# Delta scan: one chain of four heads on halves and quarters of the array, without zero padding

## The chip, the cores and the metric

The kernel runs on one core of a Trainium2 chip. The metric is the device time of one execution in microseconds (us): median of several runs. The core has a matrix engine (PE in the profile; PEld are its weight loads), a vector engine (DVE), a scalar engine (ACT), GpSimd (POOL) and a queue engine (SP) that issues DMAs. Lnnn is a line of the kernel before; lines of the changed kernel are marked as such.

## The reference

Two layers; each joins two branches that run along 512 tokens of 2048 channels. The change lies in branch A, a gated delta rule over chunks of 64 tokens, for 8 heads of 128 channels, once forwards and once backwards:

```python
def step(S, xs):
    q_c, k_c, u_c, w_c, g_c, qk_c = xs
    v_new = u_c - jnp.einsum('bhck,bhkv->bhcv', w_c, S)
    o_c = (jnp.einsum('bhck,bhkv->bhcv', q_c * jnp.exp(g_c)[..., None], S)
           + jnp.einsum('bhcs,bhsv->bhcv', qk_c, v_new))
    g_last = g_c[..., -1:]
    S = (S * jnp.exp(g_last)[..., None]
         + jnp.einsum('bhck,bhcv->bhkv', k_c * jnp.exp(g_last - g_c)[..., None], v_new))
    return S, o_c
```

`u_c` and `w_c` come from a triangular solve over the chunk; the kernel holds the inverse of that triangle times beta (`T` below) and applies it to `v - k S`. All else in a layer is large dense products: the input projection, the gated unit and projection of branch B, the merge and the output projection.

## The kernel before, in words

Dense products keep 128x128 weights in the array and stream 512 tokens. Each is three passes in split precision (L122, L123, L124), one contraction tile after another; a tile's three matmuls are called a **fill step** here. Eight weight tiles at a time come by DMA (`w_raw`), ACT makes their high part (L65) and DVE their low part (L66).

The scan, `_delta_scan`, runs over 16 steps in each layer: two groups of four heads, and eight steps `j` in each. In a step the forward direction (`d = 0`) takes chunk `j` and the backward one chunk `7 - j`; one of them lies on partitions 0 to 63 of its 128-token tile, the other on 64 to 127 (`half[d]`). Each group is split into two chains, `x = 0, 1`, of two heads. A step does, for each chain and both directions:

- **ps_T** (L807): (q | k) times the state `S`, four float32 matmuls on the whole array into one PSUM bank. Each float32 matmul stands as two instructions in the trace.
- **r_s** (L810): DVE, `v - k S`, one instruction of 64x256 for each direction. Then the state is decayed (L813, 128x512).
- **ps_V** (L821): `T` times `r_s`, two matmuls with 128 rows. `T` holds both directions' 64x64 blocks on the diagonal, zeros beside them.
- **v_z** (L824): ACT copies the new values out of PSUM, each direction to a tile of its own whose other half is zero.
- **ps_S** (L831): keys times new values, four matmuls with 128 rows of which 64 meet zeros. DVE adds them to the state (L836).
- **outputs** (L839): `a_s` times new values onto ps_T, four matmuls of 128 rows and 64 columns, into the half of the partitions of their direction. ACT copies them out while `j < 4` (L844), after that DVE adds them (L846).

The order on PE is written by hand (`manual_schedule`); each `fill.run(FILL)` puts three fill steps into it: one after the ps_T of both chains, one after both ps_V, one at the step's end. So a step has nine fill steps, 27 dense matmuls. Fill steps come from the last two of the 48 z products and from branch B's gated unit and projection; those that the scan leaves over run after it. Other engines' order is the scheduler's, with weight splits and epilogues of dense products at high priority. When a group is done, `norm` makes its head norms on ACT and DVE, and its heads leave PE by transposes, one a step (`late`).

The inputs of the scan are written to DRAM in `_delta_pre` and `_delta_inv` and loaded by the POOL queue (`load`).

Of the kernel before, what the change touches and what calls it, by code (L numbers as in the profile page):

```python
# [15 lines left out]
F32 = mybir.dt.float32  # L16
# [12 lines left out]
NH = 8  # L29
# [13 lines left out]
FILL = 3  # L43
# [4 lines left out]
# The order of the first three products.  x: loads an input tile; h: its two parts; s: its squares;  # L48
# w j,k,n: weights of product j from contraction tile k on; p j,n: the next n steps of product j.
# [31 lines left out]
def _dense(c, w, nk, hi, lo):  # L81
    """PSUM [128, 512] = w.T @ act over nk contraction tiles; w is a DRAM view [128, nk, 128]."""
# [8 lines left out]
def _weights(c, w):  # L91
    """hi and lo parts of up to eight weight tiles."""
# [10 lines left out]
class _Fill:  # L103
    """Dense products in small steps, for the places where another chain waits."""
# [11 lines left out]
def _steps(c, acc, nk, unit, hi, lo):  # L116
    """acc = w.T @ act, one contraction tile at a time; unit gives the weights from a tile on."""
# [17 lines left out]
def _sum_sq(c, ps, acc, t0, n, first):  # L135
    """Adds the sums of acc over partitions, token tiles t0 to t0 + n, onto the columns of ps [token, tile]."""
# [13 lines left out]
def _spread(c, pb, r, n):  # L150
    """pb [any partition, token] = r [token, tile]."""
# [4 lines left out]
def _rstd(c, acc, out):  # L156
    """out = (sum of acc over partitions / D + eps) ** -0.5 on every partition."""
# [8 lines left out]
def _scaled_parts(c, x, g, hi, lo):  # L166
    """Splits x*g into hi, lo."""
# [4 lines left out]
def _add_squares(c, pool, k, x, acc):  # L172
    """Adds x*x onto acc."""
# [84 lines left out]
        # c.gtok: [token in tile, t, row]; rows 0-7/32-39 exp(tot - gc), rows 64-71/96-103 g  # L258
# [9 lines left out]
def _halves(c, out, w, x, start, stop):  # L268
    """out [128, n] = w.T @ x by halves of the columns of the array, side by side."""
# [27 lines left out]
def _sincos(nc, pool, s_out, c_out, x, tag):  # L297
    """sin and cos of x by quarter turns and polynomials."""
# [18 lines left out]
    # quadrant q = n mod 4 from f = n/4 - round(n/4) in {-1/2, -1/4, 0, 1/4, 1/2}:  # L317
    # cos(pi n / 2) = 1 - 4|f| on those points, sin(pi n / 2) = sign of f on odd n
# [6 lines left out]
    # sin(pi n / 2) = 4 f (1 - cq^2)  # L325
# [13 lines left out]
def _s5(ctx, c, l):  # L339
    """S5 scan in chunks of 8 tokens; partitions are (lag, channel) or (re|im, state)."""  # L340
# [5 lines left out]
    for hf in range(2):  # L346
        with ExitStack() as es:
# [12 lines left out]
            with tc.tile_pool(name=f"s5p_{l}_{hf}", bufs=1, reuse_waits="tile") as pp:  # L360
# [17 lines left out]
                # (lam_bar - 1) / lam  # L378
# [13 lines left out]
                # b_bar: rows (re, im); b_in[0] = (b_re, b_im), b_in[1] = (b_im, b_re)  # L392
# [12 lines left out]
                # powers 0..8  # L405
# [23 lines left out]
            def gen(out, a, p, b, q, gs, d, ks, kn):  # L429
                """out [128, 4, kn, 16] = a*p + b*q over lags ks (a slice)."""  # L430
# [12 lines left out]
            # chunk inputs of the state: forward into slot n + 1, backward into slot n  # L443
# [41 lines left out]
            def kernels(jl):  # L485
                """What the outputs of a channel tile need besides the states."""
# [28 lines left out]
                # M[(s, c'), g, t, c] = K[c', g, t - s, c]  # L515
# [40 lines left out]
def _qk_norms(c, ss):  # L556
    """Inverse norms, by tokens, from the sums of squares ss [(t, k heads | q heads), token in tile]."""
# [47 lines left out]
def _delta_pre(c, l):  # L605
# [4 lines left out]
    with tc.tile_pool(name=f"dp_{l}", bufs=1, side="right", reuse_waits="tile") as wk, \  # L610
            tc.tile_pool(name=f"pp_{l}", bufs=1, space=PSUM, side="right", reuse_waits="tile") as pp:
        for h in range(NH):
            # decay factors [(chunk parity, s), direction, t, c], masked
            ps = c.psq.tile(W, F32, name="ps_d", tag="psq")
            for d in range(2):
                # tri[k, c] g[k]: k <= c forward, k >= c backward
# [15 lines left out]
            for d in range(2):  # L632
# [4 lines left out]
                # columns of chunk n: (q_e | k_e) for even n, (k_e | q_e) for odd n  # L637
# [5 lines left out]
                # in the order in which the direction takes the chunks  # L643
                nc.scalar.copy(out=c.egl[:, d, h, ::1 - 2 * d], in_=pe[:, last:SEQ:CH])
# [19 lines left out]
            for d in range(2):  # L664
# [3 lines left out]
                c.q.dma_start(out=c.d_kd[l][d, :, :, h, :].rearrange("t p x -> p t x"), in_=kd)  # L668
# [36 lines left out]
def _delta_scan(c, l, fill):  # L705
    """Both directions over the chunks, in two groups of four heads, each as two chains of two heads."""
# [3 lines left out]
    NC = 2  # L710
    with ExitStack() as es:
# [3 lines left out]
        tb = [tp.tile([128, 4, 128], F32, name=f"t_b{q}") for q in range(2)]  # L715
        # new values, zero in the half of the other direction
        vz = [[[tp.tile([128, 2, 128], F32, name=f"v_z{x}{d}{p}") for p in range(2)] for d in range(2)] for x in range(NC)]
        Sg = [[tp.tile([128, 2, 2, 128], F32, name=f"s_st{hg}{x}") for x in range(NC)] for hg in range(2)]
# [556 lines left out]
```

## Time and profile before

| | |
|---|---|
| median of 3 runs | 3102.72 us (3102.61 to 3102.72) |
| span of the profiled execution, first to last instruction | 3099.7 us |
| PE, DVE, ACT, POOL busy | 3049.4, 2307.3, 1049.6, 425.6 us |
| scan matmuls, both layers: L831, L807, L839, L821 | 61.9, 54.9, 41.2, 34.7 us |

The profiled execution is told by its span alone; its whole device time, with what lies around the span, is not in the record. The median of the runs is 3.0 us above the span. In the views, a row of the timeline merges neighbours of one line: start, time from the first start to the last end, engine, line, operation, tiles, array shape, operand, count, and in brackets the idle time before. Matmuls are pipelined, so one matmul's duration is longer than the distance to the next: distances between starts are what a block costs.

### The profile page before, as it was taken

To read this page: it belongs to the slowest core of one execution; us is meant where nothing else is said; L and a number is where in the kernel's file an instruction comes from. 1 tells how busy PE (TensorE), PEld (TensorE's weight loads), DVE (VectorE), ACT (ScalarE), POOL (GpSimd) and SP (SyncE) were. 2 spreads that over 40 slices of the span, in tenths; PEclk is the share of its full clock that TensorE was granted. 3 is DMA by queue.
4 is the path that set the end of the run, shared out by engine and by line. 5 is a ranking of instruction groups with operands and counts; after the bars stand their busy time and mean duration, and the time that the engine had idled before them with its cause. 6 is when DMAs were issued, how large, how long until landed. Compare 5 with 4: busy or idle time off the path is not lost.

```text
span 3099.7 us, 45254 instructions
## 1 busy us (share of the span) xinstructions
PE 3049.4 (98%) x17142; PEld 2442.4 (79%) x17142; DVE 2307.3 (74%) x4455; ACT 1049.6 (34%) x1441; POOL 425.6 (14%) x706
## 2 busy tenths in 40 slices
PE   9999999999999999999999999999999999999998
PEld 7777788777887888888887677877778878888887
DVE  8899969997797586543487998889959965765433
ACT  4343344333222442322223334343332224423222
POOL 1010112212101231000010102022130012300000
PEclk9999999999999999999999999999999999999999
DMA  6343446755434765754433435466564356657433
GB/s 204 93 140 105 129 153 179 214 168 157 153 119 149 223 195 178 245 169 143 148 112 96 129 103 150 137 195 193 166 181 139 119 188 191 201 187 232 154 117 114
DMA packets 199289, 493.47 MB, mean 159 GB/s; under 512 B 58336, under 2 KB 62912, under 8 KB 198048
## 3 DMA queue, kind: packets, MB, share of 16 engines
q1 hardware_dynamic: 154416, 345.84, 35.1%
q0 software_dynamic: 44512, 144.74, 15.3%
q8 instruction: 135, 2.21, 0.3%
q14 instruction: 82, 0.67, 0.1%
q10 hardware_dynamic: 144, 0.01, 0.0%
HBM read 381.64 MB, written 108.86 MB: 158 GB/s over the span
## 4 chain that ended last, share of the span: by engine, by line
PE 83%; DVE 11%; issue 3%; DMA 1%; ACT 0%; POOL 0%; SPq 0%; POOLq 0%; DVEq 0%; ACTq 0%
PE acc L122 24%; PE acc L123 24%; PE acc L124 24%; DVE w_lo L66 2%; PE ps_y L271 2%; PE ps_S L831 2%; PE ps_T L807 1%; DVE st_b L482 1%; DVE st_b L481 1%; DVE h_st L484 1%; PE ps_e L271 1%; DVE cv_y L550 1%; PE ps_et L457 1%; PE ps_T L839 1%; DVE st_a L483 1%
## 5 line engine op out<-in xcount | busy, mean ns | idle before, releaser
L122 PE MATMUL acc<-act,w_hi 128*128 128x512 f32 x3200 | 1279.0, 400 | 5.5 <-DVE cv_pre L546 3.7
L124 PE MATMUL acc<-act,w_lo 128*128 128x512 f32 x3200 | 1271.6, 397 | 3.5 <-DVE w_lo L66 3.5
L123 PE MATMUL acc<-act,w_hi 128*128 128x512 f32 x3200 | 1269.6, 397 | 0.0
L65 ACT CAST w_hi<-w_raw 128x1024 fp32r<-128x1024 f32 (+1 forms) x467 | 488.2, 1046 | 1202.1 <-PE acc L123 879.9
L66 DVE TENSOR_TENSOR w_lo<-w_raw,w_hi 128x1024 fp32r<-128x1024 f32 (+1 forms) x465 | 566.7, 1219 | 266.5 <-ACT w_hi L65 264.3
L122 PEld LDWEIGHTS acc<-act,w_hi 128*128 128x128 f32 x3200 | 603.0, 188 | 150.4 <-issue 8.4
L124 PEld LDWEIGHTS acc<-act,w_lo 128*128 128x128 f32 x3200 | 602.7, 188 | 149.4 <-issue 7.0
L123 PEld LDWEIGHTS acc<-act,w_hi 128*128 128x128 f32 x3200 | 603.3, 189 | 138.4 <-issue 5.1
L122 PE MATMUL acc<-m_l,w_hi 128*128 128x512 f32 (+1 forms) x528 | 205.0, 388 | 0.0
L123 PE MATMUL acc<-m_h,w_hi 128*128 128x512 f32 (+1 forms) x528 | 204.8, 388 | 0.0
L124 PE MATMUL acc<-m_h,w_lo 128*128 128x512 f32 (+1 forms) x528 | 204.7, 388 | 0.0
L550 DVE SCALAR_TENSOR_TENSOR cv_y<-cv_pre,cw,cv_y 128x510 f32<-128x510 f32 (+1 forms) x192 | 142.6, 746 | 7.5 <-ACT cv_y L548 5.5
L122 PEld LDWEIGHTS acc<-m_l,w_hi 128*128 128x128 f32 x528 | 99.5, 188 | 21.9
L123 PEld LDWEIGHTS acc<-m_h,w_hi 128*128 128x128 f32 x528 | 99.5, 188 | 21.8
L124 PEld LDWEIGHTS acc<-m_h,w_lo 128*128 128x128 f32 x528 | 99.5, 188 | 21.8
L693 DVE TENSOR_TENSOR x_tmp<-x_inv 128x62 f32<-128x62 f32 (+30 forms) x124 | 106.3, 857 | 2.9
L695 DVE TENSOR_TENSOR x_inv<-x_inv,x_tmp 128x62 f32<-128x62 f32 (+30 forms) x124 | 106.3, 857 | 2.7
L1072 DVE TENSOR_TENSOR z_t<-acc,rstd_b 128x512 f32<-128x512 f32 x96 | 66.0, 687 | 48.2 <-PE acc L124 47.6
L1158 DVE TENSOR_TENSOR x_res<-x_res,acc 128x512 f32<-128x512 f32 x31 | 21.3, 687 | 103.7 <-PE acc L124 86.5
L1142 DVE TENSOR_TENSOR g_in<-acc,g_in 128x512 f32<-128x512 f32 x32 | 22.1, 692 | 79.4 <-PE acc L124 79.4
L518 POOL DMA_DIRECT2D m_l<-d_k x128 | 67.3, 534 | 82.2 <-PE ps_y L271 56.1
L484 DVE TENSOR_TENSOR h_st<-h_st,st_a 128x64 f32<-128x64 f32 x256 | 70.3, 275 | 5.1
(356 smaller groups left out, 3251.0 us busy)
## 6 DMA issues: line engine op xcount, KB each, us to landing
w_raw<-in_w_in_dram SPq DMA_DIRECT2D x319, 512.0 KB, 4.0
w_raw<-in_w_out_dram SPq DMA_DIRECT2D x64, 512.0 KB, 3.9
d_keqe<-k_e POOLq DMA_DIRECT2D x32, 512.0 KB, 4.5
d_g<-z_t SPq DMA_DIRECT2D x64, 256.0 KB, 2.1
w_raw<-in_w_pb_dram SPq DMA_DIRECT2D x32, 512.0 KB, 3.7
g_in<-d_g SPq DMA_DIRECT2D x64, 256.0 KB, 3.1
w_raw<-in_w_pa_dram SPq DMA_DIRECT2D x32, 512.0 KB, 4.3
ke_s<-d_keqe POOLq DMA_DIRECT2D x56, 256.0 KB, 4.1
```

The source lines that it names most:

```text
L65: nc.scalar.copy(out=hi, in_=src)
L66: nc.vector.tensor_tensor(out=lo, in0=src, in1=hi.bitcast(F32), op=ALU.subtract)
L122: c.nc.tensor.matmul(acc, wh[:, q, :], lo(k), start=k == 0, stop=False)
L123: c.nc.tensor.matmul(acc, wh[:, q, :], hi(k), start=False, stop=False)
L124: c.nc.tensor.matmul(acc, wl[:, q, :], hi(k), start=False, stop=k == nk - 1)
L271: c.nc.tensor.matmul(out[r], w[:, r], x, start=start, stop=stop)
L484: V.tensor_tensor(out=hs(n + 1), in0=hs(n + 1), in1=a, op=ALU.add)
L518: c.q.dma_start(out=M[s_ * 16:(s_ + 1) * 16].rearrange("p g t c -> p g (t c)"), in_=c.d_k[l][j][:, :, 0:16, (7 - s_) * 16:(15 - s_) * 16]. ...
L550: nc.vector.scalar_tensor_tensor(out=y[:, o0:o1], in0=pre[:, i0:i0 + o1 - o0], scalar=cw[:, tap:tap + 1], in1=y[:, o0:o1], op0=ALU.mult, o ...
L693: V.tensor_tensor(out=t, in0=_bc(X[:, k + 1:, k:k + 1], [128, n, k]), in1=_bc(X[:, k:k + 1, 0:k], [128, n, k]), op=ALU.mult)
L695: V.tensor_tensor(out=X[:, k + 1:, 0:k], in0=X[:, k + 1:, 0:k], in1=t, op=ALU.add)
L1072: V.tensor_tensor(out=z, in0=acc, in1=c.rstd, op=ALU.mult)
```

## The change

The two chains become one chain of four heads, with one ps_T of two banks, one `r_s`, one ps_V, one state. Heads 2 and 3 of a group take the other half of the rows: `_delta_pre` writes their `a` and keys (`kd`) with the halves of the partitions swapped, each as two DMAs where one was (`store`). With that

- ps_V multiplies 64x64 blocks alone, eight matmuls for four, of 64 rows and 64 columns: at each `q` the four of them stand on four different quarters of the array;
- ps_S has 64 rows, eight matmuls as before, alternating between the two halves of the rows, whose sums go to different banks;
- the outputs have 64 rows and 64 columns, eight matmuls as before, four to a round on four quarters;
- `T` and the new values have no zero half any more, and the memsets of 10 tiles on POOL in each layer go;
- ACT copies the new values in one instruction of 128x512 for eight of 64x256 in a step (four in each chain); DVE's `r_s` is two of 64x512 for four of 64x256, the decay one of 128x1024 for two of 128x512, the additions to the outputs two of 64x512 for four of 64x256;
- the fill steps stand 2, 3, 4 in the three places instead of 3, 3, 3.

```diff
-FILL = 3
+FILLS = (2, 3, 4)
...
+        def store(out, x):
+            if h % 4 < 2:
+                c.q.dma_start(out=out, in_=x)
+            else:
+                c.q.dma_start(out=out[64:128], in_=x[0:64])
+                c.q.dma_start(out=out[0:64], in_=x[64:128])
...
-                c.q.dma_start(out=c.d_a[l][d, :, :, h, :].rearrange("t p c -> p t c"), in_=at[:, d])
+                store(c.d_a[l][d, :, :, h, :].rearrange("t p c -> p t c"), at[:, d])
...
-        tb = [tp.tile([128, 4, 128], F32, name=f"t_b{q}") for q in range(2)]
...
-            nc.gpsimd.memset(q, 0.0)
...
-            T = tb[p]
+            T = wk.tile([128, H4, CH], F32, name="t_i", tag="t_i")
...
+        def lanes(x, d):
+
+            e = x[:, d, 0:1, 0:1]
+            n = x.ap[1][0]
+            return bass.AP(tensor=e.tensor, offset=e.offset,
+                           ap=[list(x.ap[0]), [n * (1 - 2 * d) + 256, 2], [128, 2], [1, 128]])
...
-                        for h in range(2):
-                            nc.tensor.matmul(ps[:, d, h, :], ke[d][:, 2 * x + h, :], S[x][:, d, h, :],
-                                             start=d == 0 and h == 0, stop=True, skip_group_check=True)
+            systems = [(e, q, e if q < 2 else 1 - e) for q in range(H4) for e in range(2)]
+            ps = psp.tile([128, 2, H4, 128], F32, name="ps_T", tag="T")
+                for e, q, d in systems:
+                    nc.tensor.matmul(ps[:, e, q, :], ke[d][:, q, :], S[:, e, q, :],
+                                     start=q == 0, stop=True, skip_group_check=True)
...
+                    V.tensor_tensor(out=r[half[d]].rearrange("p (z h) x -> p z h x", z=2),
+                                    in0=v.rearrange("p (z h) x -> p z h x", z=2),
+                                    in1=lanes(ps[half[1 - d]], d), op=ALU.subtract)
...
+                V.tensor_tensor(out=S, in0=S, in1=_bc(c.egl[:, hg, :, :, j:j + 1], [128, 2, H4, 128]), op=ALU.mult)
+            fill.run(FILLS[0])
...
-                    nc.tensor.matmul(pv[:, h, :], T[:, 2 * x + h, :], rr[x][:, h, :], start=True, stop=True)
+            for q in range(2):
+                for h in (q, q + 2):
+                        nc.tensor.matmul(pv[half[d if h < 2 else 1 - d], d, q, :], T[half[d], h, :], r[half[d], h, :],
+                                         start=True, stop=True)
+            vv = wk.tile([128, 2, 2, 128], F32, name="v_n", tag="v_n")
+            nc.scalar.copy(out=vv, in_=pv[:, :, 0:2, :])
+            fill.run(FILLS[1])
...
-                            nc.tensor.matmul(ps[:, d, h, :], ld[d][1][:, 2 * x + h, :], vv[x][d][:, h, :],
-                                             start=True, stop=True)
+                for e, q, d in systems:
+                    nc.tensor.matmul(pS[:, e, q, :], ld[d][1][half[e], q, :], vv[half[e], d, q % 2, :],
+                                     start=True, stop=True)
...
-                        nc.tensor.matmul(pT[x][half[d], d, h, :], ld[d][0][:, 2 * x + h, :],
-                                         vv[x][d][:, h, :], start=j == 0 and h == 0, stop=True, skip_group_check=True)
+            for q in range(2):
+                for e, p, d in systems:
+                    if p % 2 == q:
+                        nc.tensor.matmul(ps[half[d], e, p, :], ld[d][0][half[e], p, :], vv[half[e], d, p % 2, :],
+                                         start=j == 0 and p in (0, 2), stop=True, skip_group_check=True)
...
-            fill.run(FILL)
+            fill.run(FILLS[2])
```

On PE, the state updates and outputs of the first step of the first layer stand like this before (`v_z` with different numbers are the chains and directions, `kd_s` and `a_s` with different numbers the directions; x2 are two matmuls):

```order
L831 MATMUL ps_S_9418<-v_z_9329,kd_s_9357 128x128 x2
L831 MATMUL ps_S_9418<-v_z_9331,kd_s_9363 128x128 x2
L839 MATMUL ps_T_9375<-v_z_9329,a_s_9359 64x128
L839 MATMUL ps_T_9375<-v_z_9331,a_s_9365 64x128
L839 MATMUL ps_T_9375<-v_z_9329,a_s_9359 64x128
L839 MATMUL ps_T_9375<-v_z_9331,a_s_9365 64x128
L831 MATMUL ps_S_9430<-v_z_9333,kd_s_9357 128x128 x2
L831 MATMUL ps_S_9430<-v_z_9335,kd_s_9363 128x128 x2
L839 MATMUL ps_T_9379<-v_z_9333,a_s_9359 64x128
```

and in the changed kernel (its L835 are the state updates, its L845 the outputs):

```order
L835 MATMUL ps_S<-v_n,kd_s_9350 128x128
L835 MATMUL ps_S<-v_n,kd_s_9356 128x128
L835 MATMUL ps_S<-v_n,kd_s_9350 128x128
L835 MATMUL ps_S<-v_n,kd_s_9356 128x128 x2
L835 MATMUL ps_S<-v_n,kd_s_9350 128x128
L835 MATMUL ps_S<-v_n,kd_s_9356 128x128
L835 MATMUL ps_S<-v_n,kd_s_9350 128x128
L845 MATMUL ps_T<-v_n,a_s_9352 64x128
L845 MATMUL ps_T<-v_n,a_s_9358 64x128 x2
L845 MATMUL ps_T<-v_n,a_s_9352 64x128 x2
L845 MATMUL ps_T<-v_n,a_s_9358 64x128 x2
L845 MATMUL ps_T<-v_n,a_s_9352 64x128
```

Two blocks of state updates and two of outputs in turn have become one of each.

On DVE, between the state updates of step `j = 4` of the first group and the subtraction of the next step, the rows before are these (`act`, `z_in` and `glu_s` belong to the gated unit of branch B):

```order
L836 TENSOR_TENSOR s_st_9337<-s_st_9337,ps_S_9869 128x512
L846 TENSOR_TENSOR o_tok_9341<-o_tok_9341,ps_T_9806 64x256 x2
L1099 TENSOR_TENSOR z_in<-z_in,glu_s 128x8x64
L836 TENSOR_TENSOR s_st_9338<-s_st_9338,ps_S_9881 128x512
L846 TENSOR_TENSOR o_tok_9342<-o_tok_9342,ps_T_9815 64x256 x2
L66 TENSOR_TENSOR act_9724<-z_in,act_9722 128x512
L810 TENSOR_TENSOR r_s_9921<-v_s_9660,ps_T_9920 64x256
L810 TENSOR_TENSOR r_s_9921<-v_s_9666,ps_T_9920 64x256
```

and in the changed kernel (its L841, L1105, L852, L816 and L820 are L836, L1099, L846, L810 and L813 before):

```order
L841 TENSOR_TENSOR s_st_9343<-s_st_9343,ps_S 128x512 x2
L1105 TENSOR_TENSOR z_in<-z_in,glu_s 128x8x64
L852 TENSOR_TENSOR o_tok_9345<-o_tok_9345,ps_T 64x512 x2
L66 TENSOR_TENSOR act_9718<-z_in,act_9716 128x512
L816 TENSOR_TENSOR r_s<-v_s_9637,ps_T 64x512
L816 TENSOR_TENSOR r_s<-v_s_9643,ps_T 64x512
L820 TENSOR_TENSOR s_st_9343<-s_st_9343,egl 128x1024
```

The additions to the outputs now all stand behind both state additions, and the whole of the next step's ps_T, which reuses the same two banks, waits for them; before, each chain had a ps_T bank of its own.

## Rows read from the trace of the kernel before

**Rows 1.** Page, part 1: busy time and share of each engine, instructions.

```profile
PE 3049.4 (98%) x17142; PEld 2442.4 (79%) x17142; DVE 2307.3 (74%) x4455; ACT 1049.6 (34%) x1441; POOL 425.6 (14%) x706
```

**Rows 2.** Timeline of PE, one scan step of the first layer (`j = 1` to `j = 2`).

```profile
1038.99 1.05 PE L821 MATMUL ps_V<-r_s,t_b 128*128 128x128 f32 x8
1039.80 0.48 PE L122 MATMUL acc<-act,w_hi 128*128 128x512 f32 x1
1040.12 0.39 PE L123 MATMUL acc<-act,w_hi 128*128 128x512 f32 x1
...
1041.98 1.05 PE L831 MATMUL ps_S<-v_z,kd_s 128*128 128x128 f32 x8
1042.96 0.66 PE L839 MATMUL ps_T<-v_z,a_s 128*64 128x128 f32 x8
1043.55 1.16 PE L831 MATMUL ps_S<-v_z,kd_s 128*128 128x128 f32 x8
...
1045.23 0.50 PE L122 MATMUL acc<-act,w_hi 128*128 128x512 f32 x1
1045.56 0.40 PE L123 MATMUL acc<-act,w_hi 128*128 128x512 f32 x1
...
1047.42 1.95 PE L807 MATMUL ps_T<-s_st,ke_s 128*128 128x128 f32 x16
```

**Rows 3.** Timeline of PE, the last step of a group: both chains' outputs together.

```profile
1116.16 1.09 PE L839 MATMUL ps_T<-v_z,a_s 128*64 128x128 f32 x16
```

**Rows 4.** Timeline of PE, 32-column matmuls of branch B between dense ones.

```profile
198.62 0.42 PE L508 MATMUL ps_k<-c_l,b_bar 128*32 128x128 f32 x8
...
215.64 0.40 PE L122 MATMUL acc<-act,w_hi 128*128 128x512 f32 x1
215.97 0.64 PE L508 MATMUL ps_k<-c_l,b_bar 128*32 128x128 f32 x16
216.54 0.50 PE L123 MATMUL acc<-act,w_hi 128*128 128x512 f32 x1
```

**Rows 5.** Line L839: weight loads of the outputs, shortest, median and longest ns.

```profile
L839 PEld LDWEIGHTS ps_T<-v_z,a_s x512: 132/137/137, 1030.6 to 2756.0; 128*64 128x64 f32 x171
```

**Rows 6.** DVE's groups, 1020 to 1240 us: busy, mean ns, idle before, releaser.

```profile
L66 DVE TENSOR_TENSOR w_lo<-w_raw,w_hi 128x1024 fp32r<-128x1024 f32 x24 | 29.4, 1223 | 23.0 <-ACT w_hi L65 23.0
L810 DVE TENSOR_TENSOR r_s<-v_s,ps_T 64x256 f32<-64x256 f32 x56 | 23.5, 420 | 14.1 <-PE ps_T L807 12.6 <-DMA a_s<-d_a 0.2
L836 DVE TENSOR_TENSOR s_st<-s_st,ps_S 128x512 f32<-128x512 f32 x24 | 16.4, 685 | 17.1 <-PE ps_S L831 16.9
L1099 DVE TENSOR_TENSOR z_in<-z_in,glu_s 128x512 f32<-128x512 f32 x8 | 9.3, 1168 | 0.1
```

**Rows 7.** Timeline of PE and DVE around three subtractions.

```profile
1035.11 1.95 PE L807 MATMUL ps_T<-s_st,ke_s 128*128 128x128 f32 x16
1036.75 0.85 DVE L810 TENSOR_TENSOR r_s<-v_s,ps_T 64x256 f32<-64x256 f32 x2
...
1134.46 0.87 DVE L810 TENSOR_TENSOR r_s<-v_s,ps_T 64x256 f32<-64x256 f32 x2
1135.38 0.71 PE L821 MATMUL ps_V<-r_s,t_b 128*128 128x128 f32 x4 [0.56 <-DVE r_s L810]
...
2698.70 1.95 PE L807 MATMUL ps_T<-s_st,ke_s 128*128 128x128 f32 x16
2700.13 0.86 DVE L810 TENSOR_TENSOR r_s<-v_s,ps_T 64x256 f32<-64x256 f32 x2
```

**Rows 8.** Waits of PE over the whole span: total us, times, longest.

```profile
PE ps_V L821 <- DVE r_s L810: 2.8, 4, 0.8
```

**Rows 9.** Timeline, first layer: the scan's first load on POOL, its first ps_V.

```profile
996.95 0.54 POOL L743 DMA_DIRECT2D v_s<-d_v  x1 [7.08 <-DMA d_ti<-l_in]
...
1026.68 1.05 PE L821 MATMUL ps_V<-r_s,t_b 128*128 128x128 f32 x8
```

**Rows 10.** POOL's groups over the whole span: the stores of the keys.

```profile
L668 POOL DMA_DIRECT2D d_kd<-k_d x32 | 24.0, 753 | 32.4 <-DVE k_d L666 21.2 <-DVE st_a L483 6.6 <-DMA m_l<-d_k 1.7
```

More of the change, by code (lines that the diff above doesn't have):

```diff
@@ L642, in _delta_pre @@
                 last = CH - 1 if d == 0 else 0
-                nc.scalar.copy(out=c.egl[:, d, h, ::1 - 2 * d], in_=pe[:, last:SEQ:CH])
+                nc.scalar.copy(out=c.egl[:, h // 4, d if h % 4 < 2 else 1 - d, h % 4, ::1 - 2 * d], in_=pe[:, last:SEQ:CH])
                 c.q.dma_start(out=c.d_keqe[l][d, :, :, h, :].rearrange("n p x -> p n x"),
@@ L667, in _delta_pre @@
                                 in1=_bc(c.gtok[:, :, 32 * d + h:32 * d + h + 1], [128, 4, 128]), op=ALU.mult)
-                c.q.dma_start(out=c.d_kd[l][d, :, :, h, :].rearrange("t p x -> p t x"), in_=kd)
+                store(c.d_kd[l][d, :, :, h, :].rearrange("t p x -> p t x"), kd)
 def _delta_inv(c, l):
@@ L749, in load @@
             for d in range(2):
[L750 to L752 removed]
+                c.q.dma_start(out=T[half[d]], in_=c.d_ti[l][d, hs, n_[d]].rearrange("h s c -> s h c"))
             return T, ke, dict(token)
         def norm(hg):
[L757 to L783 removed]
@@ L784, in norm @@
-            return late
+            ot = og[hg]
+            ms = tp.tile([128, 4, H4], F32, name=f"o_ms{hg}")
+            for t in range(4):
+                sq = wk.tile([128, H4, 128], F32, name="o_sq", tag=f"o_sq{t % 2}", bufs=1)
+                nc.scalar.activation(out=sq, in_=ot[:, t], func=AF.Square)
+                V.tensor_reduce(out=ms[:, t], in_=sq, axis=AX.X, op=ALU.add)
+            rq = c.rq[:, :, hg * 4:hg * 4 + 4]
+            f = tp.tile([128, 4, H4], F32, name=f"o_f{hg}")
@@ new lines, in norm @@
+            V.tensor_tensor(out=f, in0=rq, in1=rq, op=ALU.mult)
+            V.tensor_tensor(out=f, in0=f, in1=ms, op=ALU.mult)
+            V.tensor_scalar(out=f, in0=f, scalar1=1.0 / 128, scalar2=EPS, op0=ALU.mult, op1=ALU.add)
+            _rsqrt(nc, tp, ms, f, f"o_rt{hg}")
+            V.tensor_tensor(out=f, in0=ms, in1=rq, op=ALU.mult)
+            for h in range(0, H4, 2):
+                V.tensor_tensor(out=ot[:, :, h:h + 2], in0=ot[:, :, h:h + 2],
+                                in1=_bc(f[:, :, h:h + 2].unsqueeze(3), [128, 4, 2, 128]), op=ALU.mult)
@@ new lines, in head @@
+            def head(h):
+                pt = c.psq.tile([128, 4, 128], F32, name="ps_o", tag="psq")
+                for t in range(4):
+                    nc.tensor.transpose(pt[:, t, :], ot[:, t, h, :], c.ident)
+                of = wk.tile([128, 4, 128], F32, name="o_t", tag=f"o_sq{h % 2}", bufs=1)
+                nc.vector.tensor_scalar(out=of, in0=pt, scalar1=c.hng, scalar2=None, op0=ALU.mult)
+                c.q.dma_start(out=c.d_o[l][hg * 4 + h], in_=of.rearrange("p t x -> p (t x)"))
@@ L786, in _delta_scan @@
+            return [lambda h=h: head(h) for h in range(H4)]
+        def lanes(x, d):
[3 more added lines that the diff above has]
+                           ap=[list(x.ap[0]), [n * (1 - 2 * d) + 256, 2], [128, 2], [1, 128]])
         late = []
@@ L847, in _delta_scan @@
-            fill.run(FILL)
+            systems = [(e, q, e if q < 2 else 1 - e) for q in range(H4) for e in range(2)]
+            ps = psp.tile([128, 2, H4, 128], F32, name="ps_T", tag="T")
+            r = wk.tile([128, H4, 128], F32, name="r_s", tag="r_s", bufs=1)
+            if j:
+                for e, q, d in systems:
+                    nc.tensor.matmul(ps[:, e, q, :], ke[d][:, q, :], S[:, e, q, :],
+                                     start=q == 0, stop=True, skip_group_check=True)
@@ new lines, in _delta_scan @@
+            for d in range(2):
+                v = ld[d][2][half[d]]
+                if j == 0:
+                    V.tensor_copy(out=r[half[d]], in_=v)
+                else:
+                    V.tensor_tensor(out=r[half[d]].rearrange("p (z h) x -> p z h x", z=2),
+                                    in0=v.rearrange("p (z h) x -> p z h x", z=2),
+                                    in1=lanes(ps[half[1 - d]], d), op=ALU.subtract)
+            if 0 < j < NCH - 1:
+                V.tensor_tensor(out=S, in0=S, in1=_bc(c.egl[:, hg, :, :, j:j + 1], [128, 2, H4, 128]), op=ALU.mult)
@@ new lines, in _delta_scan @@
+            fill.run(FILLS[0])
+            pv = psp.tile([128, 2, H4, 128], F32, name="ps_V", tag="W")
+            for q in range(2):
+                for h in (q, q + 2):
+                    for d in range(2):
+                        nc.tensor.matmul(pv[half[d if h < 2 else 1 - d], d, q, :], T[half[d], h, :], r[half[d], h, :],
+                                         start=True, stop=True)
+            vv = wk.tile([128, 2, 2, 128], F32, name="v_n", tag="v_n")
+            nc.scalar.copy(out=vv, in_=pv[:, :, 0:2, :])
@@ new lines, in _delta_scan @@
+            fill.run(FILLS[1])
+            if j < NCH - 1:
+                pS = psp.tile([128, 2, H4, 128], F32, name="ps_S", tag="W")
+                for e, q, d in systems:
+                    nc.tensor.matmul(pS[:, e, q, :], ld[d][1][half[e], q, :], vv[half[e], d, q % 2, :],
+                                     start=True, stop=True)
+                for e in range(2):
+                    if j == 0:
+                        nc.scalar.copy(out=S[:, e], in_=pS[:, e])
+                    else:
+                        V.tensor_tensor(out=S[:, e], in0=S[:, e], in1=pS[:, e], op=ALU.add)
@@ new lines, in _delta_scan @@
+            for q in range(2):
[3 more added lines that the diff above has]
+                                         start=j == 0 and p in (0, 2), stop=True, skip_group_check=True)
+            for d in range(2):
+                o = ot[half[d], t_[d]].rearrange("p (z h) x -> p z h x", z=2)
+                if j < NCH // 2:
+                    nc.scalar.copy(out=o, in_=lanes(ps[half[d]], d))
+                else:
+                    V.tensor_tensor(out=o, in0=o, in1=lanes(ps[half[d]], d), op=ALU.add)
@@ L854, in _delta_scan @@
             f()
-            fill.run(FILL)
+            fill.run(FILLS[0])
 def _start(c, tiles, x_in, g, hi, lo, ssq):
@@ L1029, in hybrid_encoder_kernel @@
     c.gpart = const.tile([128, 2, 4, 16], F32, name="gpart")
-    c.egl = const.tile([128, 2, NH, NCH], F32, name="egl")
+    c.egl = const.tile([128, 2, 2, 4, NCH], F32, name="egl")
     c.rq = const.tile([128, 4, NH], F32, name="rq")
```

76 lines of the change are left out of this document (3 added, 73 removed).

## The prediction, made before the changed kernel ran

> **What bounds the kernel now.** I read the page first: PE is busy for 3049.4 of 3099.7 us [rows 1], with DVE next at 74%. So time is won only where PE's own work gets shorter, and lost only where PE is made to wait. Next the timeline of PE over one scan step [rows 2]. In the run of dense matmuls from 1040.12 to 1041.98 eight starts lie 0.2325 us apart. The scan's blocks stand between such runs without a gap, and the list of waits has only 2.8 us, in four waits, of ps_V for `r_s` [rows 8]. The scan is therefore not held up by its chain of engines; it costs what its matmuls cost, and that is read from distances between starts:
>
> - ps_V: 1038.99 to 1039.80, and the dense matmul behind it is followed after 0.32 instead of 0.23: 0.81 + 0.09 = 0.90 us for 8 instructions, 0.112 each. ps_T, 16 instructions, is 1.79 by that.
> - State updates and outputs together: 1041.98 to 1045.23, and 0.10 more behind (0.33 for 0.23): 3.35 us. The state updates take 16 x 0.112 = 1.79 of it.
> - Outputs on half the columns: 16 in one block last 1.09, 8 last 0.66 [rows 2, 3], so eight more cost 0.43, 0.054 each: two halves of the columns run side by side, and a pair costs what one full matmul costs. 16 x 0.054 = 0.86.
> - What is left, 3.35 - 1.79 - 0.86 = 0.70, is two visits to the half-column shape: 0.35 for going there and back.
>
> **The change, part by part.** No row of this trace shows two matmuls on different halves of the rows at once, so the gain has two ends: side by side as the columns do, or in turn. What speaks for side by side is how far the columns go: with 32 columns, 16 instructions last 0.64 and 8 last 0.42 [rows 4], 0.0275 each. That is four at once at 0.11 a round. I take side by side, with the same 0.11, and let the other end be a rival.
>
> - *ps_V on quarters*: 16 instructions in 4 rounds. The block of 16 with four at once has that very form [rows 4]: it starts 0.10 late (215.64 to 215.97, 0.33 for 0.23), takes 0.57 to the next start, and the dense matmul behind costs 0.10 as it does behind the outputs: 0.77. Against 0.90 this saves 0.13.
> - *State updates on halves of the rows*: 8 rounds of 0.112, 0.90. *Outputs on quarters*: 4 rounds of 0.11, 0.44. The shape now changes three times here (full, half rows, quarters, full) where it changed four times; at 0.175, half a visit, 0.52. Together 1.86 against 3.35: 1.49 saved.
> - ps_T and the 27 dense matmuls of a step stay as they are.
>
> That is 1.62 us a step. Of the 32 steps, 28 have a state update: 45.4. The four last steps of a group save 0.13 in ps_V and, for outputs that stood in one block already (0.86 + 0.35 = 1.21, now 0.77), 0.44: 2.3. **Saved on PE: 47.7 us.** Between 0 and 0.2 for a change of shape, the 0.52 moves by -0.52 to +0.08; over 28 steps that is -15 to +2.
>
> Now what comes back as waiting.
>
> - *The wait for the subtraction.* Six dense matmuls now stand between ps_T and ps_V, and no second chain. PE reaches ps_V 0.03 + 0.32 + 5 x 0.2325 + 0.10 = 1.61 after ps_T's last start. DVE needs both banks for each of its two instructions, so it starts after the last matmul's end (0.27 later: 1.05 for 8 starts of 0.112 [rows 2]). An instruction of 64x256 takes 0.42 and one with 512 columns 0.685 [rows 6], so two take 1.38. The way from DVE to PE takes 0.05 (1134.46 + 0.87 to 1135.38 [rows 7]), and I take as much for the way to DVE. 0.27 + 0.05 + 1.38 + 0.05 = 1.75: PE waits 0.14 in each of the 28 steps, 3.9 us.
> - *DVE not free.* Before, the second chain hid a late start: PE's cover was nine dense matmuls and half of ps_T. Of the 28 first subtractions ten begin late, because DVE is still in a weight split, a head's epilogue or the gated unit. The first: ps_T from 1035.11, its eighth matmul ends 7 x 0.112 + 0.27 = 1.05 later, the subtraction begins at 1036.75, 0.59 late. The last: 2698.70 and 2700.13, 0.38 late [rows 7]. The ten come to 7.2 us. With 0.14 missing already, all of it is PE's now: 7.2 us.
> - *ps_T for one chain.* It reuses the banks that the additions to the outputs read. From the last state update's start DVE needs 0.27 + 0.05 + 4 x 0.69 + 0.05 = 3.13; PE needs the outputs (0.44 + 0.35) and 12 dense matmuls (2.8), 3.6. That holds with 0.5 to spare; with `z_in`'s 1.17 between, as in the order after step 4, it falls short by 0.7. I take that for two steps in each layer at 0.6: 2.4 us. Nothing if DVE is ahead; 12 steps of 1.2, 14, at worst.
> - *The copy of the new values* is one ACT instruction of 512 columns for several of 256. No row has it; by DVE's 0.69 for 512 columns, with 0.27 + 0.05 ahead, and even behind a split as long as DVE's 1.22, it is done after 2.2, under the nine dense matmuls behind ps_V (0.32 + 8 x 0.2325 + 0.10 = 2.3). Nothing; a second instruction ahead of it would show.
> - The four waits of 2.8 us [rows 8] are the same waits and are in the terms above: -2.8.
> - *`store`*: 16 more DMAs on POOL in each layer, at 0.753 for an issue [rows 10] 12 us of POOL. The scan's first load is issued at 996.95 and its first ps_V stands at 1026.68 [rows 9], so 29.7 us cover it; without them it would be 24 us for both layers. The memsets go from POOL ahead of those loads. Nothing.
>
> Sum: -47.7 + 3.9 + 7.2 + 2.4 - 2.8 = -37.0. The profiled span goes from 3099.7 to 3062.7; the median lies 3.0 above the span, so **3066 us**, 1.2% faster.
>
> [...] The weight loads of the outputs last 0.137 [rows 5], yet the pairs of column halves follow each other at 0.11, so a load runs while a matmul of the same rows runs. [...]
>
> **The rivals.**
>
> 1. *DVE always late.* If a weight split (1.22 [rows 6]) stood ahead of every subtraction, the second term would be 28 x 1.22 = 34 in place of 7.2: 3066 + 27 = 3093. For it: one chain has no partner, and DVE's work now comes within a shorter step. Against: 18 of 28 subtractions began on time, and DVE's work in the scan gets less.
> 2. *Halves of the rows take turns* (the other side). Then ps_V is 16 x 0.054 + 0.35 = 1.21 for 0.90, +9.9 over 32 steps; the state updates stay at 1.79 and the outputs at 0.86; the changes of shape save 0.17 in 28 steps, -4.8. PE's work grows by 5.1, the waits of 3.9 and 7.2 come on top, 2.8 go: **3116 us**, slower. Break-even is where the rows give 30% of the overlap. For it: no row shows it. Against: columns do it fourfold.
> 3. *Loads show in each round of quarters*: 8 x 0.137 x 32 steps = 35 us back: 3101, no change. Against: rows 5 beside rows 2.
> 4. *Everything covered*: no wait at all, 3102.7 - 47.7 - 2.8 = 3052.2. It is the lower edge of the forecast, not a case of its own.
>
> **How the numbers follow.** The forecast, all rounds side by side and waits of 0 to 25 us, has 0.70; rival 1 0.12, rival 2 0.13, rival 3 0.03; 0.02 stay for what I don't see. The range goes from 3050 (all covered, cheaper changes of shape) to 3096 (rival 1 with a little more), and leaves out rivals 2 and 3 and the rest, 0.18. About 0.2%, 6 us, can be told from no change. Faster: forecast, rival 1 and a part of the rest, 0.83. Same: rival 3 and edges, 0.05. Slower: rival 2, 0.12.
>
> **What the profile after would show.** Right: the block of 16 state updates lasts about 1.2 us with starts 0.056 apart on average; ps_V's 16 and the outputs' 16 about 0.64 each; a step is some 10.9 us instead of 12.3; and the waits name ps_V behind `r_s`, some 11 us. Wrong: the 16 state updates take 1.8 (rival 2); rounds of quarters lie 0.25 apart (rival 3); waits of ps_V or ps_T for DVE above 25 us (rival 1).

## The result, and the profile after

The changed kernel takes 3081.27 us (median of 4 runs, 3080.46 to 3085.16) beside 3102.66 for the kernel before: 0.9934 of its time, 95% interval 0.992 to 0.9948, 21.4 us less. The forecast was 3066 (3050 to 3096): the sign and the range hold, the size is 58% of the 36.7 us that were forecast. The profiled execution has a span of 3083.3 us (3099.7 before), the slowest of the four. In the runs that list both, the time lies about 1.8 us above the span, and not 3.0 as was taken for the kernel before: its profile is of an execution some 1.2 us below the median, the one after of an execution 3.9 above, so the two spans differ by only 16.4 us.

The saving on PE is there. Timeline of PE in the changed kernel, from one ps_V to the next (its L827 is ps_V, L835 the state updates, L845 the outputs, L808 ps_T); it answers to [rows 2]:

```profile
1035.05 0.83 PE L827 MATMUL ps_V<-r_s,t_i 64*64 64x128 f32 x16
1035.81 0.50 PE L122 MATMUL acc<-act,w_hi 128*128 128x512 f32 x1
...
1038.10 1.16 PE L835 MATMUL ps_S<-v_n,kd_s 64*128 64x128 f32 x16
1039.19 0.67 PE L845 MATMUL ps_T<-v_n,a_s 64*64 64x128 f32 x16
1039.79 0.50 PE L122 MATMUL acc<-act,w_hi 128*128 128x512 f32 x1
...
1042.68 1.95 PE L808 MATMUL ps_T<-s_st,ke_s 128*128 128x128 f32 x16
1044.38 0.47 PE L122 MATMUL acc<-act,w_hi 128*128 128x512 f32 x1
...
1045.95 0.83 PE L827 MATMUL ps_V<-r_s,t_i 64*64 64x128 f32 x16
```

Read distances between starts: 16 state updates 1.09 us, 16 outputs 0.60, ps_V 0.76, and the step 10.90 (1035.05 to 1045.95) where it was 12.31. The forecast was 1.2, 0.64, 0.64 and 10.9. ps_V's block holds 0.16 of waiting between the two halves of `r_s`; where DVE is early it too lasts 0.60.

What was not forecast stands in the list of waits of PE, total us, times, longest; it answers to [rows 8]:

```profile
PE ps_T L808 <- ACT o_tok L850: 8.3, 2, 4.3
...
PE ps_T L808 <- issue: 4.2, 6, 1.0
...
PE ps_V L827 <- DVE r_s L816: 3.6, 12, 0.4
...
PE ps_o L781 <- DVE o_tok L775: 2.6, 2, 1.3
```

The first line is new in kind: ps_T waits for ACT's copies of the outputs (`o_tok`), once in each layer, at `j = 3` to `j = 4`. Timeline of ACT and PE around the first of the two:

```profile
1059.22 0.62 ACT L65 CAST act<-ys_in 128x512 fp32r<-128x512 f32 x1 [4.59 <-DMA ys_in<-d_y]
...
1061.61 0.67 PE L845 MATMUL ps_T<-v_n,a_s 64*64 64x128 f32 x16
...
1064.68 0.62 ACT L65 CAST act<-ys_in 128x512 fp32r<-128x512 f32 x1 [4.23 <-DMA ys_in<-d_y]
1065.20 1.04 ACT L65 CAST w_hi<-w_raw 128x1024 fp32r<-128x1024 f32 x1
1066.78 0.72 ACT L1083 ACTIVATE z_t<-z_t,chp 128x512 f32<-128x512 f32 x1 [0.54 <-DVE z_t L1078]
1067.41 0.60 ACT L65 CAST act<-ys_in 128x512 fp32r<-128x512 f32 x1
...
1068.03 1.17 ACT L850 COPY o_tok<-ps_T 64x512 f32<-64x512 f32 x2
...
1069.26 3.79 PE L808 MATMUL ps_T<-s_st,ke_s 128*128 128x128 f32 x16 [4.01 <-ACT o_tok L850]
```

The outputs are done at 1062.3. ACT could copy them then, but it stands in a cast of branch B that waits 4.23 us for its load `ys_in`; three more instructions follow, and the copies begin at 1068.03. ps_T, which reuses those banks, waits 4.01 us. And its 16 instructions then last 3.79 us where they last 1.95 elsewhere. Busy time in windows around it (busy us and count of PE, PEld, DVE, ACT, POOL, then the granted clock, DMA share, GB/s):

```profile
1065.30:1067.90 2.60, 0.00 (x0) 0.00 (x0) 2.54 (x4) 2.06 (x3) 0.00 (x0) 1.00 1.04 311
1067.90:1069.20 1.30, 0.00 (x0) 0.00 (x0) 1.30 (x3) 1.26 (x4) 0.00 (x0) 0.50 1.13 305
1069.20:1074.70 5.50, 5.45 (x21) 5.06 (x22) 2.73 (x5) 1.14 (x3) 1.06 (x2) 0.50 0.87 242
1074.70:1080.00 5.30, 5.30 (x61) 3.79 (x60) 3.30 (x4) 2.22 (x3) 1.25 (x2) 1.00 0.49 151
```

The granted clock falls from 1.00 to 0.50 while PE stands idle, and stays there for 5.5 us of work. The second layer shows the same: 4.27 us of waiting up to 2603.58, then 3.4 us at a mean clock of 0.54 (there it is still 1.00 in the idle time, 0.65 in the first microsecond of work and 0.50 in the next two).

The second line of the waits, `issue`, is explained by DVE's rows at such a place:

```profile
1080.08 1.28 DVE L841 TENSOR_TENSOR s_st<-s_st,ps_S 128x512 f32<-128x512 f32 x2
1081.28 1.19 DVE L1105 TENSOR_TENSOR z_in<-z_in,glu_s 128x512 f32<-128x512 f32 x1
1082.36 1.37 DVE L852 TENSOR_TENSOR o_tok<-o_tok,ps_T 64x512 f32<-64x512 f32 x2
...
1083.83 2.02 PE L808 MATMUL ps_T<-s_st,ke_s 128*128 128x128 f32 x16 [1.01 <-issue]
```

ps_T starts 0.10 us after the additions to the outputs end (1083.73), and `z_in` stands ahead of them, as it does in the other two such steps of this layer. The profile names no releaser; the place in time suggests one, and e10_pool below tests it.

So the theory is: PE's work shrank as forecast, and late loads of branch B took a part of it back, by ACT's queue and by the clock. The rival: in a step that is 1.4 us shorter, ACT and DVE simply have too much to do, and the loads only look like the cause.

### The profile page after: what moved, and what is told of

It reads as the page before. It is cut to its first block, busy times and chain, and to the rows that moved or that the text cites. A ratio compares the mean times of both kernels' runs of the same rounds, so it can differ in the third digit from the quotient of the medians.

```text
span 3083.3 us, 45415 instructions
## 1 busy us (share of the span) xinstructions
PE 3014.7 (98%) x17398; PEld 2387.5 (77%) x17398; DVE 2288.5 (74%) x4299; ACT 1016.7 (33%) x1310; POOL 435.8 (14%) x718
## 3 DMA queue, kind: packets, MB, share of 16 engines
q0 software_dynamic: 45024, 144.74, 15.3%
```

## The experiments

Edits are to the changed kernel unless said otherwise; times are medians, ratios are to the kernel before. "Scans" are the spans from the first ps_V to the last outputs of both layers together, in the profiled execution: 360.0 us in the changed kernel. Where the fill steps stand 3, 2, 4, one fill step more of each scan lies ahead of its first ps_V, so the two stretches hold six dense matmuls fewer; that is 1.4 us (6 x 0.2325) and no gain.

**e12_again**: the changed kernel, unedited.

> The changed kernel once more, unedited, beside the others. Theory (the late loads are a property of the order of the queues, not of one execution): ps_T waits 4 us for ACT's copies once in each layer again, and the time is 3081. Rival (the wait was that of one slow execution, the profiled one lay 4 us above the others): the waits are below 2 us, time 3077 or less in most runs.

3080.97 us (0.9933, 0.9919 to 0.9947). The waits recur at the same place, though shorter; the list of waits of PE:

```profile
PE ps_T L808 <- ACT o_tok L850: 5.7, 2, 3.0
PE ps_T L808 <- issue: 4.2, 6, 1.0
```

So they belong to the order of the queues, while their length varies: 2.65 and 3.04 us in this execution, whose scans are 355.8 us. The rival's low time did not come.

**e1_y6**: buffers of their own for the loads.

```diff
-                y = c.tmp.tile([128, SEQ], F32, name="ys_in", tag="x_in", bufs=XIN)
+                y = c.yp.tile([128, SEQ], F32, name="ys_in", tag="y_in")
...
+            with tc.tile_pool(name=f"yin_{l}", bufs=6, reuse_waits="tile") as c.yp:
```

> The loads of branch B's second halves (ys_in) get six buffers of their own instead of three that they share. Theory (late loads: ACT stands in a cast that waits for a load, the copies of the outputs stand behind it, ps_T waits for them, and the clock is granted at half after the wait): the two waits of ps_T for ACT's copies (4.2 and 4.3 us, 8.3 together) go below 1 us, no stretch of the scan has a granted clock of 0.5, and the time falls by about 13.5 us, from 3081.3 to 3068. Rival (at this place ACT and DVE simply have too much work for a step that is 1.4 us shorter, and the loads only look like the cause): ps_T still waits 2 us or more in each layer and the time stays above 3076. Between the two, if the waits shrink but DVE's state additions are then what is late: 3070 to 3075.

3105.89 us (1.0012, 1.0003 to 1.0021): slower than either kernel. The time lies where the rival had it, for a reason that neither theory had. The list of waits of PE, its longest line and the one in question:

```profile
PE acc L122 <- ACT w_hi L65: 23.5, 4, 11.5
...
PE ps_T L808 <- ACT o_tok L850: 1.6, 2, 1.1
```

The wait for the copies went from 8.3 to 1.6 us and the scans from 360.0 to 349.9, but ahead of each scan the dense matmuls now wait for weights. Timeline of SP in the first layer:

```profile
1006.77 7.30 SPq L1091 DMA_DIRECT2D ys_in<-d_y  x5
...
1018.73 2.72 SPq L96 DMA_DIRECT2D w_raw<-in_w_in_dram  x2
```

With buffers free early, the loads went ahead of the weights in SP's queue, at 1006 instead of 1055 us; PE stood from 1021 to 1031.5 while the DMA share was 1.02. The edit moved the cost. Whether the time falls with the waits in the scan was still open.

**e6_gate**: buffers of their own for five of the loads, which are held back by a one-element copy from the first dense tile inside the scan.

```diff
+                    if j == 46:
+                        c.ys = [c.yp.tile([128, SEQ], F32, name=f"ys_in{q}") for q in range(5)]
+                        for y in c.ys:
+                            nc.scalar.copy(out=y[0:1, 0:1], in_=z[0:1, 0:1])
...
+                y = c.ys[j - 3] if j > 2 else c.tmp.tile([128, SEQ], F32, name="ys_in", tag="x_in", bufs=XIN)
```

> Again buffers of their own for the y loads (five beside the three shared ones, so that none of the eight waits for a buffer), but each of the five loads now waits for a copy of one element from the gate tile 46, which is the first dense work of the scan: so they cannot go ahead of the weights any more as in e1_y6, where they were issued at 1006 us and TensorE waited 10.5 us for weights. Theory (late loads cost 13.5 us, and e1_y6 lost its gain to the weights alone): the two scans last 350 us together as in e1_y6 (360.0 in the changed kernel), no wait for weights ahead of them, the waits of ps_T for ACT's copies below 2 us, time 3081.3 - 10 = 3071. Rival (the loads only change places with the weights of the gated unit, and the same wait returns there): 3077 to 3083.

3072.39 us (0.9907, 0.9893 to 0.9921), 8.9 below the changed kernel; scans 347.95. The groups of ps_T and ps_V (busy, mean ns, idle before, what ended it), first of the changed kernel; before, ps_T had 54.9 us and waited for nothing:

```profile
L808 PE MATMUL ps_T<-s_st,ke_s 128*128 128x128 f32 x448 | 58.4, 286 | 12.5 <-ACT o_tok L850 8.3 <-issue 4.2
...
L827 PE MATMUL ps_V<-r_s,t_i 64*64 64x128 f32 x512 | 27.7, 283 | 3.7 <-DVE r_s L816 3.6
```

and of e6_gate:

```profile
L808 PE MATMUL ps_T<-s_st,ke_s 128*128 128x128 f32 x448 | 55.0, 276 | 4.3 <-issue 4.3
...
L827 PE MATMUL ps_V<-r_s,t_i 64*64 64x128 f32 x512 | 28.0, 283 | 5.0 <-DVE r_s L816 4.8
```

The 8.3 us for ACT's copies are gone, and ps_T's busy time is 3.4 lower; the granted clock is 1.00 on average in each scan, where it was 0.98 and 0.99. For these waits the rival is refuted: but for five copies of one element only the time of the loads changed, and ACT kept up. The waits for DVE (4.3 and 5.0 us here) are still there.

**e11_before_gate**: the same edit in the kernel before (three buffers).

> The kernel before with the edit of e6_gate (three y loads get buffers of their own behind gate tile 46; there is room for three). In the kernel before ACT also stands 3.7 us in a cast that waits for a y load, but no wait of TensorE follows from it. Theory (the late loads cost something only where one chain of longer instructions has no cover for them): no change, 3099 to 3103. Rival (the loads cost TensorE as much before, in a place that the list of waits does not show): 3095 or less.

3102.30 us (0.9999, 0.999 to 1.0008): nothing. ACT's longest wait for such a load falls from 3.71 to 1.9 us, and PE had not waited for it. Timeline of ACT in the kernel before:

```profile
1056.89 1.51 ACT L844 COPY o_tok<-ps_T 64x256 f32<-64x256 f32 x4
1062.11 0.62 ACT L65 CAST act<-ys_in 128x512 fp32r<-128x512 f32 x1 [3.71 <-DMA ys_in<-d_y]
...
1064.30 1.54 ACT L824 COPY v_z<-ps_V 64x256 f32<-64x256 f32 x4 [0.37 <-PE ps_V L821]
```

The late load was there before, but it stood behind the copies of the outputs, and the copies of the new values that came next still had to wait 0.37 us for PE. In the changed kernel the cast stands ahead of the copies of the outputs. So the place in ACT's order made it harmless. Whether a second chain's banks would also have covered it, no run tells.

**e2_324 and e7_gate324**: more cover for the subtraction, alone and with the gated loads.

```diff
-FILLS = (2, 3, 4)
+FILLS = (3, 2, 4)
```

> The fill steps stand 3, 2, 4 instead of 2, 3, 4: nine dense matmuls between ps_T and ps_V, six between ps_V and the state updates. Theory (ps_V's waits for the subtraction, 10.5 us, are missing cover, 0.16 us in the common step): cover grows by 3 x 0.2325 = 0.70 us, which hides the common wait and most of the longer ones; r's waits fall to 1 to 3 us, and the copy of the new values (0.59 us and 0.4 for the ways) still fits under 1.6 us. Time 3073, 8 below the 3081 of the changed kernel. Rival: the cover taken from behind ps_V shows as waits of the state updates for the new values, or the waits move to the additions: 3079 to 3083.

> The loads as in e6_gate and the fill steps 3, 2, 4. In e4_y6_324 the two scans lasted 342.9 us together, 17.1 less than in the changed kernel, and what it lost was the wait for weights ahead of them. Theory: 3081.3 - 17 = 3064, waits of ps_V for the subtraction below 1 us. Rival (the wait of e2_324's kind, the copy of the new values behind ACT's casts, is there without late loads too): 3070 to 3076.

Alone 3079.59 us (0.9928, 0.9916 to 0.9941), which the changed kernel's interval overlaps: the rival's time. Three of its waits of PE:

```profile
PE acc L122 <- DVE act L66: 5.5, 5, 2.0
PE ps_S L835 <- ACT v_n L830: 3.9, 3, 2.9
...
PE ps_T L808 <- ACT o_tok L850: 2.8, 1, 2.8
```

The copy of the new values now stands behind the same cast that waits for its load (2.87 us up to 2596.78, in the second layer), and the dense matmuls wait for `act`, which is made from the same loads. With the gated loads, 3064.81 us (0.9882, 0.9868 to 0.9895), 7.6 below e6_gate. Its groups:

```profile
L808 PE MATMUL ps_T<-s_st,ke_s 128*128 128x128 f32 x448 | 55.0, 276 | 4.2 <-issue 4.2
...
L827 PE MATMUL ps_V<-r_s,t_i 64*64 64x128 f32 x512 | 24.1, 282 | 0.6 <-DVE r_s L816 0.5
```

ps_V's busy and idle time together fall from 33.0 to 24.7: the third fill step takes back 8.3 us of the waits for the subtraction. Without the gated loads, where ACT's queue can stop, only 1.7 us of it show in the time.

**e4_y6_324**: e1_y6 and e2_324 together.

> Both edits together, six buffers for the loads and fill steps of 3, 2, 4. If the two costs are independent: 3081.3 - 13.5 - 8 = 3060. If they are the same waits seen twice (what one removes comes back at the other place): no better than 3066.

3093.76 us (0.9975, 0.9965 to 0.9985), by e1_y6's wait for weights (11.3 and 10.0 us). The scans are 342.9 us, 17.1 less than in the changed kernel; without the 1.4 for the moved fill steps that is 15.7, 5.6 more than e1_y6 alone gains there. So the gains are not the same waits seen twice.

**e8_prio**: the scan's DVE and ACT work in e7_gate324 at a higher priority (the same line stands ahead of the subtractions, the copy of the new values and the state additions).

```diff
+            with c.tc.high_priority(offset=2 * PRIO):
+                for d in range(2):
+                    o = ot[half[d], t_[d]].rearrange("p (z h) x -> p z h x", z=2)
```

> e7_gate324 with the scan's own work on DVE and ACT (subtraction, decay, copies, additions) ahead of the weight splits, z_in and the casts wherever both are ready by the order's planner. Theory (ps_T still waits some 4 us a run for additions that stand behind z_in, and 3 for copies): those waits go below 2 us and the time is 3059 to 3062. Rival (the splits that are put back make the dense matmuls wait for weights): 3064 to 3072, with new waits of the dense matmuls for w_lo.

3065.95 us (0.9883, 0.9868 to 0.9898): no change, and inconclusive on its question, since the order kept `z_in` ahead where it matters. Timeline of DVE:

```profile
1075.49 1.28 DVE L844 TENSOR_TENSOR s_st<-s_st,ps_S 128x512 f32<-128x512 f32 x2
1076.69 1.19 DVE L1113 TENSOR_TENSOR z_in<-z_in,glu_s 128x512 f32<-128x512 f32 x1
1077.77 1.40 DVE L856 TENSOR_TENSOR o_tok<-o_tok,ps_T 64x512 f32<-64x512 f32 x2
```

The wait `issue` of 4.2 us stayed.

**e10_pool**: `z_in` leaves DVE, on top of e7_gate324.

```diff
-                    V.tensor_tensor(out=z.rearrange("p (n t) -> p t n", t=8), in0=z.rearrange("p (n t) -> p t n", t=8),
+                    nc.gpsimd.tensor_tensor(out=z.rearrange("p (n t) -> p t n", t=8), in0=z.rearrange("p (n t) -> p t n", t=8),
                                     in1=s.rearrange("p (t n) -> p t n", t=8), op=ALU.mult)
```

> e7_gate324 with one more edit: the product that makes z_in in the gated unit (1.17 us of DVE, eight times in a layer) runs on POOL. Theory (ps_T's waits of 0.5 to 1.0 us in three steps of each layer, 4.2 in all, come from z_in ahead of the additions to the outputs, as in e7_gate324 and also in e8_prio, whose order kept z_in ahead): these waits go below 0.5 us in all and the time is 3061 (3064.8 less 4). Rival (POOL's queue: z_in stands among the scan's loads and waits for DVE's product, so a load of the scan comes late and ps_T, ps_V or the outputs wait for it): 3065 or more, with waits that name a DMA or POOL; if each of eight loads shows by 1 us, 3075.

3054.25 us (0.9845, 0.9832 to 0.9859), the fastest here, 10.6 below e7_gate324 where 4 were expected. Its groups, and `z_in` on POOL (min, median and max ns):

```profile
L808 PE MATMUL ps_T<-s_st,ke_s 128*128 128x128 f32 x448 | 54.7, 275 | 0.0
...
L827 PE MATMUL ps_V<-r_s,t_i 64*64 64x128 f32 x512 | 23.0, 282 | 1.1 <-DVE r_s L816 1.1
```

```profile
L1109 POOL TENSOR_TENSOR z_in<-z_in,glu_s x8: 1512/1582/1714, 1073.2 to 1140.4; 128x512 f32<-128x512 f32 x8
```

ps_T's 4.2 us are gone, and with them 3.2 us in which the heads' transposes (ps_o) waited for DVE's norm, a wait that was not in the expectation. The scans are 329.7 us against 338.8. POOL takes 1.58 us for what DVE did in 1.17, and inside the scans no wait of PE names POOL or a DMA, against the rival. One wait is new: the state updates wait 1.2 us for ACT's copy of the new values. What this does not tell apart is `z_in`'s place in the order from DVE's load in general: both were taken away.

**e3_noswap**: no swapped halves; ps_V and outputs meet two quarters at a time, the state updates stay on both halves, and ACT copies the new values in two instructions.

```diff
-            systems = [(e, q, e if q < 2 else 1 - e) for q in range(H4) for e in range(2)]
+            systems = [(e, q, e) for q in range(H4) for e in range(2)]
...
-            for q in range(2):
-                for h in (q, q + 2):
-                    for d in range(2):
-                        nc.tensor.matmul(pv[half[d if h < 2 else 1 - d], d, q, :], T[half[d], h, :], r[half[d], h, :],
+            for q in range(H4):
+                for d in range(2):
+                    nc.tensor.matmul(pv[half[d], d, q, :], T[half[d], q, :], r[half[d], q, :],
```

> One part undone: no heads have their halves of the rows exchanged, so ps_V and the outputs meet only two quarters at a time (eight rounds of two instead of four of four); state updates stay on both halves of the rows, and ACT copies the new values in two instructions. Theory (four quarters at once give 0.44 us in each of ps_V and the outputs, in 32 steps): PE's blocks of ps_V and outputs last 1.04 to 1.1 instead of 0.60, 28 us in all, of which some 5 come back because the longer blocks cover more of the waits: 3100 to 3109. Rival (quarters give nothing beyond halves, and the gain is the single chain alone): 3079 to 3085.

3100.36 us (0.9999, 0.999 to 1.0008). Without the quarters nothing is left of the change. Timeline of PE (its L822 is ps_V, L831 the state updates, L839 the outputs):

```profile
1036.36 1.24 PE L822 MATMUL ps_V<-r_s,t_i 64*64 64x128 f32 x16
...
1039.83 1.16 PE L831 MATMUL ps_S<-v_n,kd_s 64*128 64x128 f32 x16
1040.92 1.09 PE L839 MATMUL ps_T<-v_n,a_s 64*64 64x128 f32 x16
```

From block start to the next start, ps_V comes to 41.3 us over the 32 steps and the outputs to 33.5, against 27.7 and 19.1: 28.0 us more, the expected sum. Of it 19.1 reach the time, since ps_T's waits fall from 12.5 to 4.7 us under the longer blocks.

**e5_turn**: the state updates of one half of the rows ahead of those of the other.

```diff
-                for e, q, d in systems:
+                for e, q, d in sorted(systems):
```

> One part undone in order alone: in the state updates the eight matmuls of one half of the rows stand ahead of the eight of the other, instead of alternating. Nothing else changes. Theory (two halves of the rows run side by side only where neighbours in the order meet different halves): the block of 16 lasts 1.8 to 2.0 us again instead of 1.09, some 0.8 us in each of 28 steps, 22 to 25 us, of which a few come back because DVE's first state addition starts half a block earlier: 3098 to 3106. Rival (the gain of the state updates does not come from the neighbours, or matmuls of the second half overtake): the block stays near 1.1 and the time at 3079 to 3083.

3091.82 us (0.9966, 0.9954 to 0.9979), 10.6 above the changed kernel: between the two forecasts. Timeline of PE:

```profile
1040.75 1.71 PE L835 MATMUL ps_S<-v_n,kd_s 64*128 64x128 f32 x16
1042.39 0.67 PE L845 MATMUL ps_T<-v_n,a_s 64*64 64x128 f32 x16
```

The block takes 1.64, not 1.8 to 2.0. Starts in it lie 0.112 apart at both ends, as on the whole array, but where the second half follows the first, several come in pairs, 0.004 to 0.006 apart. So the second half begins beside the last ones of the first. 0.547 us in 28 steps is 15.3. Of it 10.6 us reach the time, since ps_T's waits fall from 12.5 to 6.0. The expectation gave an earlier start of DVE's first addition as the reason, and that did not happen: in an undisturbed step it starts 0.1 us behind the whole block, 1.75 us after the block's start where it was 1.21. PE comes to ps_T 0.55 us later, and finds more of the same work on DVE and ACT done.

## Why the prediction was right, and where its size was off

- **Saved on PE, 47.7 us**: right, and shown from both ends. The blocks came out at 1.09 and 0.60 against 1.2 (0.90 and a change of shape) and 0.64. With nearly all waits removed, PE is busy for 327.5 us in e10_pool's scans, where it was 374.2 before: 46.7 less, or 45.3 without the 1.4 for the moved fill steps.
- **Rival 1** (DVE always late, 3093): refuted, the waits for the subtraction are some 11 us and not 34.
- **Rivals 2 and 3** (halves in turn, loads in each round): refuted by the step of 10.90 us. A block of 16 on quarters takes 0.60, four rounds with the change of shape; the rounds follow at 0.11 although a weight load there lasts 0.13.
- **The wait for the subtraction, 3.9 + 7.2**: right. From the last dense start ahead of ps_V to the first behind it, the 32 blocks of the changed kernel take 40.1 us, where 32 of the shortest (0.916) would take 29.3: 10.8 us of waiting beside the 11.1 forecast. More cover took back 8.3 of such waits (e6_gate beside e7_gate324).
- **ps_T for one chain, 2.4 us**: this is the step that failed. It priced DVE's additions alone, 0.7 short where `z_in`'s 1.17 stands between them, and took that for two steps a layer at 0.6. Six waits of 4.2 us came of that (up to 1.0, in three steps a layer). The larger part it left out: while `j < 4` it is ACT that frees the banks, and in ACT's queue a cast that waits for a load stood ahead of the copies. The prediction priced ACT only for the copy of the new values, and asked what stands ahead of it by its duration, not by what it waits for. e6_gate shows the cost: 8.9 us in the medians; in the profiled scans 12.1, of which PE's idle time is 7.4 (19.7 to 12.3) and PE's longer busy time 4.7 (340.3 to 335.7).
- **The heads' transposes** had no place in the sum. They wait 2.6 us for DVE's norm and 0.7 for DVE to free the bank that they write (`o_t`), and did not wait before.
- **The clock** had none either. [rows 2] stand at a granted clock of 1.00, and a sum of waits took each at its own length.
- **Together**, as an estimate from these numbers: 8.9 us for the late loads, 1.8 for more additions than priced, 3.3 for the transposes and 2.4 less saved on PE make 16.4; the median missed the forecast by 15.3.
- **The copy of the new values, nothing**: right with nine matmuls of cover (0.5 us in all), and the text's own condition, "a second instruction ahead of it would show", was met in e2_324 with six.
- **Everything covered, 3052**: not a case of the changed kernel, but e10_pool reaches 3054.25 by removing the three waits one after another.
- **`store`, nothing**: the first ps_V came at 1023.7 and 1026.2 in two executions, 1026.68 before [rows 9]: no sign of a cost.

What stays open: the start of the first scan lies between 1023.1 and 1028.8 us in the profiled executions of kernels whose edits lie behind it (e1_y6 and e4_y6_324 apart; e3_noswap, whose edit also undoes `store`, lies within), in two of the changed kernel at 1023.7 and 1026.2; no run told what moves it. It is why the profiled execution of e12_again, with 4.2 us less in its scans, has a span only 1.9 us shorter, and it blurs by as much what the spans of two profiles differ by.

## What to carry to other kernels

When two chains become one, ask of every buffer that the pair had twice who frees it, and read the whole queue of that engine up to the freeing instruction: here a cast that waited 3.71 us for its DMA behind it, in the kernel before, made PE wait for nothing, and one that waited 4.23 us ahead of it, in the changed kernel, made PE wait 4.01 us. A forecast of PE's own time from distances between starts came within 2.4 us of 47.7; the waits were where most of the error lay. Give a late load buffers and also a lower bound on its time: with buffers alone (e1_y6) the loads went ahead of the weights, for which PE waited 23.5 us; with both (e6_gate) the time fell by 8.9 us.

## What the runs showed of the hardware that was not expected

- Two waits of PE cost more than their length. After those of 4.0 and 4.3 us in the changed kernel the granted clock was 0.5 for 5.5 us of work and a mean of 0.54 over 3.4. In e12_again a wait of 2.65 us was followed by 6.6 us and more at full clock, and one of 3.04 by a mean of 0.57 over 4 us. In e2_324 the clock stayed full for 8 us behind a wait of 2.75 us, and behind waits of 1.15 and 1.99 us soon after it was 0.63 on average over 4 us. So in these runs the length of one wait does not tell what the clock does behind it.
- In e5_turn matmuls on the two halves of the rows run side by side although the program does not alternate them, those next to the border: 16 take 1.64 us in turn and 1.09 alternating, where 16 starts 0.112 apart would take 1.79.
- In the changed kernel four quarters at once, with new weights in each round, go at about 0.11 us a round: the starts of four outputs lie 0.006 to 0.007 apart and the next four follow, while a weight load there lasts 0.13.
